# A four-layer trunk on one Trainium2 core: the RWKV chains of four tiles become two chains of two tiles in step

## The chip, the cores and the metric

The kernel runs on one core of a Trainium2 chip. Its engines are TensorE (PE, matmuls, with its weight loads as a row of their own, PEld), VectorE (DVE), ScalarE (ACT), GpSimd (POOL) and SyncE (SP), whose queue issues the DMAs. The metric is the device time of one execution, in microseconds. The time before is the median of three runs, and beside it stands one execution taken with the hardware profiler, from which all rows come.

## What is computed

Two layers of a decoder trunk on 256 positions of width 2048, each followed by a SwiGLU FFN, all between RMS norms, in float32. The second layer is an RWKV-7 time mix with 32 heads of 64. Its heart is a recurrence over the positions (cut from the reference):

```python
def step(state, inp):
    r_t, d_t, k_t, v_t, kk_t, a_t = inp
    sk = jnp.einsum("bhvk,bhk->bhv", state, kk_t)
    state = (state * d_t[:, :, None, :]
             - sk[..., None] * (kk_t * a_t)[:, :, None, :]
             + v_t[..., None] * k_t[:, :, None, :])
    return state, jnp.einsum("bhvk,bhk->bhv", state, r_t)
...
y = ((y - mu) * lax.rsqrt(var + RWKV_LN_EPS)).reshape(b, s, d)
y = y * ln_w + ln_b
bonus = jnp.sum(r_h * k_h * r_k, axis=-1, keepdims=True) * v_h
return ((y + bonus.reshape(b, s, d)) * gate) @ w_o
```

## The kernel before

The recurrence is computed in chunks of 64 positions (four of them), for a tile of 128 channels (two heads) at a time: 16 tiles, eight pairs q of two tiles, four groups g of two pairs. All this is one stage of the kernel, some 490 us long, in which several kinds of work are woven together:

- `rec_pre(q)` projects receptance and key of a pair (lines 1294 to 1299): 2 x 16 blocks of 6 matmuls into a `pw` bank each, evacuated by ScalarE into `r_t` (L1296, two buffers) and `k_t` (L1298, one buffer). The weights come as `raw` by DMA (L371, three buffers) and are split into `whi` (ScalarE, L273) and `wlo` (VectorE, L274).
- `rec_load(q)` loads four prepared tensors of the pair, `rec_head(q)` makes from them and `r_t`, `k_t`, for each tile, `KR`, `BK`, `AB`, `KG`, `BT` and `V` (L1349 to L1397). `KR`, `AB`, `KG`, `V` and `BT` have five buffers (`NH = 5`), `BK` has one. Its matmuls go to the three banks of tag `ph`.
- `rec_solve(g)` is the chain of a group of four tiles. It inverts triangular matrices by doubling: for each of four levels two steps, each with 64 matmuls of 32 x 32 (`mul`, L1413; the profile has two records of each), evacuated by VectorE (`W`, L1427), or by ScalarE and VectorE (`Tm`, `Rc`, L1431 and L1432). Two joins follow (L1439, L1450), and then the four chunks in turn: `X` (L1466, L1469, evacuated by ScalarE at L1471), `E` (L1476, L1477), and the state `S` (L1488, L1490, L1492 or L1494). At the end come the outputs of the two pairs, one after the other (L1509 to L1535): matmuls, a norm over each head, the bonus and the gate (L1531). The chain's matmuls go to the three banks of tag `pc`; its tiles `R`, `Rc`, `Tm`, `W`, `X` and `S` have one buffer each.
- `rec_gate(q)` loads the pair's gate into `gt` (one buffer, L1544).
- `wo_part(i)` adds part of the output projection (first of tiles 0 to 7, then of 8 to 11), with two `pw` banks at a time (L317, L322, L323). The last part follows after the stage.

PSUM has eight banks: two of `pw`, three of `ph`, three of `pc`. The tasks get due times: pair q's projections from q - 1.6 to q - 0.55, its head from q - 0.5 to q + 0.45, group g's chain from 2g + 1.5 for `LS` = 1.5, its gates `LS` - 0.5 behind; `weave` runs them step by step in the order of these times. From the order in which they are written and a model of the engines, the library then sets the order on every engine, which is fixed when the kernel is built. In it an instruction that is written earlier goes first among those that are ready.

Of the kernel before, what the change touches and what calls it, by code (L numbers as in the profile page):

```python
# [11 lines left out]
F32 = mybir.dt.float32  # L12
# [91 lines left out]
def tile_trunk(ctx: ExitStack, tc: tile.TileContext, A, out, dbg=None):  # L104
# [1156 lines left out]
    rebank(2, {"ph": 3, "pc": 3})  # L1261
    rcx, rcp = phase("rec")
    RB = {"r_t": 2, "KR": NH, "AB": NH, "KG": NH, "V": NH, "BT": NH, "bon": 3, "pd": 2}
# [137 lines left out]
    def rec_solve(g):  # L1401
# [3 lines left out]
        U4 = range(4)  # L1405
        UC = [(u, ch) for u in U4 for ch in range(4)]

        def mul(L, X):

            v_ = c32(pbank("pc"))  # L1410
            for u, ch in UC:
                for b, s_ in enumerate(QS):
                    mm(v_[s_, 4 * u + ch, :], lhsT=L(b, u, ch), rhs=X[s_, 4 * u + ch, :], start=True, stop=True)  # L1413
            return v_


        Rw = Sr([P, 16, 64], "R")
        for u in U4:
            tt(Rw[:, 4 * u : 4 * u + 4, :], AB[u][:, :, 0:64], bcn("rm1t", 4), ALU.mult)
        R = Sr([P, 16, 32], "Rc")  # L1420
        tt(R, Rw[:, :, 0:32], Rw[:, :, 32:64], ALU.add)
        Tm = Sr([P, 16, 32], "Tm")
        nc.vector.transpose(flat(Tm), flat(R))
        for lv in (2, 4, 8, 16):
            W = Sr([P, 16, 32], "W")
            p_ = mul(lambda b, u, ch: AB[u][QS[b], ch, 32 * (b % 2) : 32 * (b % 2) + 32], Tm)
            tt(W, p_, bcn(f"rl{lv}", 16), ALU.mult)  # L1427
            yield 1
            p_ = mul(lambda b, u, ch: R[QS[b], 4 * u + ch, :], W)
            Tm, R = Sr([P, 16, 32], "Tm"), Sr([P, 16, 32], "Rc")  # L1430
            act(flat(Tm), flat(p_), AF.Copy)  # L1431
            nc.vector.transpose(flat(R), flat(p_))  # L1432
            yield 1

        Rc, R = R, Sr([P, 16, 64], "R")
        p_ = c32(pbank("pc"))
        for u, ch in UC:
            for b in (0, 2):
                mm(p_[QS[b + 1], 4 * u + ch, :], lhsT=AB[u][QS[b], ch, 32:64], rhs=Tm[QS[b], 4 * u + ch, :],  # L1439
                   start=True, stop=True)  # L1440
        W = Sr([P, 16, 32], "W")
        act(W[QS[1]], p_[QS[1]], AF.Copy)
        nc.vector.tensor_copy(W[QS[3]], p_[QS[3]])
        tt(R.rearrange("p c (b n) -> p c b n", b=2), Rc.unsqueeze(2).to_broadcast([P, 16, 2, 32]),
           C("bd32").rearrange("p (b n) -> p b n", b=2).unsqueeze(1).to_broadcast([P, 16, 2, 32]), ALU.mult)
        yield 1
        p_ = c32(pbank("pc"))
        for u, ch in UC:
            for b in (0, 2):
                mm(p_[QS[b], 4 * u + ch, :], lhsT=W[QS[b + 1], 4 * u + ch, :], rhs=Rc[QS[b + 1], 4 * u + ch, :],  # L1450
                   start=True, stop=True)
        act(R[QS[0], :, 32:64], p_[QS[0]], AF.Copy)
        nc.vector.tensor_copy(R[QS[2], :, 32:64], p_[QS[2]])
        yield 1

        Ss = Sr([P, 3, 4, 64], "S")
        E2 = [Sr([P, 2, 4, 64], t) for t in ("Tm", "Rc")]

        def E(ch):
            return E2[ch // 2][:, ch % 2]  # L1460

        for ch in range(4):
            px = c64(pbank("pc")[:, :T])
            for u in U4:
                for s_ in HS:
                    mm(px[s_, u, :], lhsT=KG[u][s_, ch, 0:64], rhs=V[u][s_, ch, :], start=True, stop=ch == 0)  # L1466
                if ch:
                    for s_ in HS:
                        mm(px[s_, u, :], lhsT=KR[u][s_, ch, 0:64], rhs=Ss[s_, ch - 1, u, :], start=False, stop=True)  # L1469
            X = Sr([P, 4, 64], "X")  # L1470
            act(X, px, AF.Copy)  # L1471
            yield 1
            pe = c64(pbank("pc")[:, :T])
            for u in U4:
                for s_ in HS:
                    mm(pe[s_, u, :], lhsT=R[s_, 4 * u + ch, :], rhs=X[s_, u, :], start=True, stop=True)  # L1476
            nc.vector.tensor_copy(E(ch), pe)  # L1477
            if ch in (1, 2):
                dec = Sr([P, 4, 64], "X")
                for u in range(2):  # L1480
                    tt(dec[:, 2 * u : 2 * u + 2, :], Ss[:, ch - 1, 2 * u : 2 * u + 2, :],
                       pds[u][:, :, ch].unsqueeze(2).to_broadcast([P, 2, 64]), ALU.mult)
            yield 1
            if ch < 3:
                pS = c64(pbank("pc")[:, :T])
                for u in U4:
                    for s_ in HS:
                        mm(pS[s_, u, :], lhsT=BT[u][s_, ch, 1, :], rhs=V[u][s_, ch, :], start=True, stop=False)  # L1488
                    for s_ in HS:
                        mm(pS[s_, u, :], lhsT=BT[u][s_, ch, 0, :], rhs=E(ch)[s_, u, :], start=False, stop=True)  # L1490
                if ch:
                    tt(Ss[:, ch], dec, pS, ALU.add)  # L1492
                else:
                    nc.vector.tensor_copy(Ss[:, 0], pS)  # L1494
                yield 1
        for v in range(2):
            pr2 = 2 * g + v
            py = pbank("pc")
            y4 = py.rearrange("p (u c n) -> p u c n", u=2, n=64)
            for w_ in range(2):  # L1500
                u = 2 * v + w_
                for i in range(3):
                    for ch in range(4):
                        if i == 1 and ch == 0:
                            continue
                        for s_ in HS:
                            lhs, rhs = ((V[u][s_, ch, :], KG), (Ss[s_, max(ch - 1, 0), u, :], KR),
                                        (E(ch)[s_, u, :], AB))[i]
# [8 lines left out]
            r0, sq = flat(Sr([P, 2, T], "W")), Sr([P, 2, 2 * T], "R")[:, 0, :]  # L1517
            act(r0, pv, AF.Abs_reciprocal_sqrt, bias=epst[:, 2:3], scale=1.0 / 64)
            act(sq, r0, AF.Square)
            yield 1  # L1520
            stt(sq, pv, 64 * 64e-5, sq, ALU.add, ALU.mult)
            act(sq, sq, AF.Copy, scale=-0.5 / 64, bias=1.5)
            tt(r0, py, r0, ALU.mult)
            tt(r0, r0, sq, ALU.mult)
            for j in range(2):
                c = 2 * pr2 + j
# [64 lines left out]
    for g in range(4):  # L1591
        t = 2 * g + 1.5
        tasks.append((t, t + LS, 28, rec_solve(g)))
# [51 lines left out]
```

## Time and profile before

| | |
|---|---|
| time, median of three runs | 2665.96 us (2663.95 to 2678.07) |
| profiled execution | 2662.39 us, of which the span from first to last instruction 2660.6 us |
| mean granted TensorE clock | 0.978 of 2.4 GHz |
| PE busy | 2569.1 us (97% of the span) |
| PEld, DVE, ACT busy | 2225.8, 1540.4, 1315.0 us |
| the stage of the change | about 1397 to 1891 us after the span's start |

Busy time of PE counts a matmul until its modelled end. Idle time of an engine is put down to what released the instruction that follows it: another engine's line, a DMA, or "issue", where the profile shows no releaser.

### The profile page before, as it was taken

What the parts mean: (1) busy time and instruction counts of PE and PEld (TensorE: products, weight loads), DVE (VectorE), ACT (ScalarE), POOL (GpSimd) and SP (SyncE); (2) the same over time, 40 slices, a digit from 0 to 9 for tenths busy, and PEclk for the clock granted to TensorE, in tenths of its full rate; (3) what the DMA queues carried; (4) which work ended last, traced back from release to release, by engine and by line L of the source; (5) the groups of instructions that cost most, each with busy time, mean ns of one, the idle gap of its engine ahead of it and who ended that gap; (6) DMA issues with size and microseconds to landing.
All of it is one profiled execution on the core that took longest, in us unless ns stands there. A gap on an engine that the chain in (4) does not pass through costs nothing.

```text
span 2660.6 us, 50321 instructions
## 1 busy us (share of the span) xinstructions
PE 2569.1 (97%) x21102; PEld 2225.8 (84%) x21102; DVE 1540.4 (58%) x2183; ACT 1315.0 (49%) x1953; POOL 33.3 (1%) x99
## 2 busy tenths in 40 slices
PE   8999999999999999998999998889899999999998
PEld 8999988788888888887999897777688888888886
DVE  7866666655444554458776574664655444555455
ACT  6665545544444434445577473553554444443443
POOL 1000000000000000000000000000000000000000
PEclk9999999999999999998999998899899999999999
DMA  7544546666566656655587442533366666666665
GB/s 208 148 121 129 175 144 198 179 185 194 183 192 187 193 187 190 190 186 176 177 278 219 130 133 67 171 99 126 112 185 190 190 192 193 187 193 194 190 184 164
DMA packets 275331, 461.49 MB, mean 173 GB/s; under 512 B 23752, under 2 KB 89216, under 8 KB 274336
## 3 DMA queue, kind: packets, MB, share of 16 engines
q1 hardware_dynamic: 274720, 458.12, 56.6%
q8 instruction: 165, 2.70, 0.4%
q14 instruction: 62, 0.51, 0.1%
q0 software_dynamic: 384, 0.16, 0.0%
HBM read 441.93 MB, written 16.29 MB: 172 GB/s over the span
## 4 chain that ended last, share of the span: by engine, by line
PE 92%; DVE 3%; ACT 2%; DMA 2%; issue 1%; SPq 0%; DVEq 0%; ACTq 0%
PE pw L317 27%; PE pw L322 20%; PE pw L323 20%; PE pw L320 7%; PE pw L319 7%; PE pc L1413 2%; PE ph L1364 1%; PE pc L1509 1%; DVE wlo L274 1%; DMA raw<-in_rwkv_w_o_dram 1%; PE pc L1476 1%; ACT whi L273 1%; PE pw L1176 1%; PE pc L1490 0%; PE pc L1469 0%
## 5 line engine op out<-in xcount | busy, mean ns | idle before, releaser
L274 DVE TENSOR_TENSOR wlo<-raw,whi 128x1024 fp32r<-128x1024 f32 (+1 forms) x814 | 975.9, 1201 | 881.1 <-ACT whi L273 877.4
L273 ACT ACTIVATE whi<-raw 128x1024 fp32r<-128x1024 f32 (+1 forms) x814 | 844.4, 1040 | 971.3 <-PE pw L323 795.9
L322 PE MATMUL pw<-wlo,xs_hi 128*128 128x512 f32 x1664 | 651.9, 392 | 0.0
L323 PE MATMUL pw<-whi,xs_lo 128*128 128x512 f32 x1664 | 648.8, 391 | 0.0
L317 PE MATMUL pw<-whi,xs_hi 128*128 128x512 f32 x1664 | 599.6, 393 | 0.7 <-ACT fw L465 0.7
L322 PEld LDWEIGHTS pw<-wlo,xs_hi 128*128 128x128 f32 x1664 | 313.6, 188 | 65.0 <-issue 0.7
L317 PEld LDWEIGHTS pw<-whi,xs_hi 128*128 128x128 f32 x1664 | 313.1, 188 | 65.5 <-issue 1.0
L323 PEld LDWEIGHTS pw<-whi,xs_lo 128*128 128x128 f32 x1664 | 313.2, 188 | 65.3 <-issue 0.7
L317 PE MATMUL pw<-xs_hi,whi 128*128 128x256 f32 x1168 | 334.1, 288 | 4.2 <-ACT xs_hi L1148 3.6
L319 PE MATMUL pw<-xs_lo,whi 128*128 128x256 f32 x1168 | 332.5, 286 | 0.0
L320 PE MATMUL pw<-xs_hi,wlo 128*128 128x256 f32 x1168 | 329.7, 287 | 0.3 <-DVE wlo L274 0.3
L323 PE MATMUL pw<-whi,hidl 128*128 128x512 f32 x704 | 276.7, 393 | 0.0
L322 PE MATMUL pw<-wlo,hidh 128*128 128x512 f32 x704 | 275.9, 392 | 0.0
L317 PE MATMUL pw<-whi,hidh 128*128 128x512 f32 x704 | 250.2, 393 | 0.0
L317 PEld LDWEIGHTS pw<-xs_hi,whi 128*128 128x128 f32 x1168 | 224.1, 192 | 6.0 <-ACT xs_hi L1148 3.9
L319 PEld LDWEIGHTS pw<-xs_lo,whi 128*128 128x128 f32 x1168 | 224.0, 192 | 0.9 <-DVE xs_lo L1138 0.3
L320 PEld LDWEIGHTS pw<-xs_hi,wlo 128*128 128x128 f32 x1168 | 221.9, 192 | 1.2 <-DVE wlo L274 0.5
L323 PEld LDWEIGHTS pw<-whi,hidl 128*128 128x128 f32 x704 | 132.3, 188 | 30.0
L317 PEld LDWEIGHTS pw<-whi,hidh 128*128 128x128 f32 x704 | 132.3, 188 | 29.3
L322 PEld LDWEIGHTS pw<-wlo,hidh 128*128 128x128 f32 x704 | 132.3, 188 | 29.0
L320 PE MATMUL pw<-xr_hi,wlo 128*128 128x256 f32 x288 | 82.1, 285 | 2.4 <-DVE wlo L274 2.3
L317 PE MATMUL pw<-xr_hi,whi 128*128 128x256 f32 x288 | 82.1, 285 | 2.0 <-ACT whi L273 2.0
(582 smaller groups left out, 2502.0 us busy)
## 6 DMA issues: line engine op xcount, KB each, us to landing
raw<-in_ffn_w_gate_dram SPq DMA_DIRECT2D x176, 512.0 KB, 3.8
raw<-in_ffn_w_up_dram SPq DMA_DIRECT2D x176, 512.0 KB, 3.7
raw<-in_ffn_w_down_dram SPq DMA_DIRECT2D x176, 512.0 KB, 3.7
raw<-in_hyb_w_in_dram SPq DMA_DIRECT2D x80, 512.0 KB, 3.7
raw<-in_hyb_w_out_dram SPq DMA_DIRECT2D x32, 512.0 KB, 3.9
raw<-in_rwkv_w_v_dram SPq DMA_DIRECT2D x32, 512.0 KB, 4.4
raw<-in_rwkv_w_r_dram SPq DMA_DIRECT2D x32, 512.0 KB, 4.5
raw<-in_rwkv_w_k_dram SPq DMA_DIRECT2D x32, 512.0 KB, 4.2
```

Source lines behind the costliest of these rows:

```text
L273: behind(act(hi, src, AF.Copy), after[0])
L274: behind(tt(lo, src, hi.bitcast(F32), ALU.subtract), after[1])
L317: mm(dst, lhsT=lh, rhs=rh, start=start, stop=False, skip_group_check=True)
L319: mm(dst, lhsT=lh, rhs=rl, start=False, stop=False, skip_group_check=True)
L320: mm(dst, lhsT=ll, rhs=rh, start=False, stop=stop, skip_group_check=True)
L322: mm(dst, lhsT=lh, rhs=rl, start=False, stop=False, skip_group_check=True)
L323: mm(dst, lhsT=ll, rhs=rh, start=False, stop=stop, skip_group_check=True)
L1176: mm(ps[:96, 0, :], lhsT=wt[:, (c + j) % 8, :], rhs=xm[:, j, :], start=c + j == 0, stop=c + j == ND - 1)
L1364: mm(g[:, ch * P : (ch + 1) * P], lhsT=bdk[:, ch, i, :], rhs=KR[:, ch, :], start=True, stop=True)
L1413: mm(v_[s_, 4 * u + ch, :], lhsT=L(b, u, ch), rhs=X[s_, 4 * u + ch, :], start=True, stop=True)
L1476: mm(pe[s_, u, :], lhsT=R[s_, 4 * u + ch, :], rhs=X[s_, u, :], start=True, stop=True)
L1509: mm(y4[s_, w_, ch, :], lhsT=lhs, rhs=rhs[u][s_, ch, 64:128], start=i + ch == 0, stop=i == 2, skip_group_check=True)
```

## The change

Each group's chain becomes two chains, of two tiles each, which are written step by step in turn. Each has its own tiles (`R0`, `R1` and so on, half as wide) and its own two PSUM banks (`pc0`, `pc1`); `ph` has two banks left. All matmuls stay; each evacuation is half as wide, and there are twice as many. The outputs of both pairs are written in turn as well, each by single tiles of 256 columns: squares and head sums in `W`, `Tm` and `Rc`, then the norm, the bonus and, for both tiles together, the gate. The key gets a second buffer. The gate loads use the one buffer of `BK` in place of `gt`. A chain's slot `LS` is 1.3 in place of 1.5, and its instructions count as if they were written 100 places earlier.

```diff
-    rebank(2, {"ph": 3, "pc": 3})
+    rebank(2, {"ph": 2, "pc0": 2, "pc1": 2})
-    RB = {"r_t": 2, "KR": NH, "AB": NH, "KG": NH, "V": NH, "BT": NH, "bon": 3, "pd": 2}
+    RB = {"k_t": 2, "r_t": 2, "KR": NH, "AB": NH, "KG": NH, "V": NH, "BT": NH, "bon": 3, "pd": 2}
...
+        R, Ss, E = [None, None], [None, None], [None, None]
+        def chain(v):
+            UC = [(u, ch) for u in range(2) for ch in range(4)]
+            ab, kr, kg, bt, vv = (x[2 * v : 2 * v + 2] for x in (AB, KR, KG, BT, V))
+            pc = f"pc{v}"
+            def Sv(shape, tag, dt=F32):
+                return Sr(shape, tag + str(v), dt)
...
-            W = Sr([P, 16, 32], "W")
-            p_ = mul(lambda b, u, ch: AB[u][QS[b], ch, 32 * (b % 2) : 32 * (b % 2) + 32], Tm)
-            tt(W, p_, bcn(f"rl{lv}", 16), ALU.mult)
+                W = Sv([P, 8, 32], "W")
+                p_ = mul(lambda b, u, ch: ab[u][QS[b], ch, 32 * (b % 2) : 32 * (b % 2) + 32], Tm)
+                tt(W, p_, bcn(f"rl{lv}", 8), ALU.mult)
...
-            X = Sr([P, 4, 64], "X")
-            act(X, px, AF.Copy)
+                X = Sv([P, 2, 64], "X")
+                act(X, px, AF.Copy)
...
-            sq = Sr([P, 2, T], "W")
-            act(flat(sq), py, AF.Square)
-            pv = pbank("pc")
-            hl = Sr([P, 2, 2 * T], "R", F32R)
-            headsum(pv, flat(sq), hl[:, 0, :], hl[:, 1, :])
...
+            pv = pbank(pc)
             for j in range(2):
+                sl = slice(j * T, (j + 1) * T)
+                sq = Sv([P, T], "W")
+                act(sq, py[:, sl], AF.Square)
+                headsum(pv[:, sl], sq, Sv([P, T], "Tm", F32R), Sv([P, T], "Rc", F32R))
+            yield 1
+            for j in range(2):
+                sl = slice(j * T, (j + 1) * T)
                 c = 2 * pr2 + j
+                r0, sq = Sv([P, T], "W"), Sv([P, T], "Tm")
+                act(r0, pv[:, sl], AF.Abs_reciprocal_sqrt, bias=epst[:, 2:3], scale=1.0 / 64)
+                act(sq, r0, AF.Square)
+                stt(sq, pv[:, sl], 64 * 64e-5, sq, ALU.add, ALU.mult)
+                act(sq, sq, AF.Copy, scale=-0.5 / 64, bias=1.5)
+                tt(r0, py[:, sl], r0, ALU.mult)
+                tt(r0, r0, sq, ALU.mult)
+                act(r0, r0, AF.Identity, scale=pcol(3, 32 + c), bias=pcol(3, 48 + c))
+                tt(bon[:, sl], r0, bon[:, sl], ALU.add)
             tt(bon, bon, flat(gate[pr2]), ALU.mult)
...
+        for f in (chain, output):
+            for _ in zip(f(0), f(1)):
+                yield 1
...
-        gate[pr2] = Sr([P, 2, T], "gt")
+        gate[pr2] = Sr([P, 2, T], "BK")
...
-    LS = 1.5
+    LS = 1.3
...
-        tasks.append((t, t + LS, 28, rec_solve(g)))
+        tasks.append((t, t + LS, 28, rec_solve(g), 100))
```

## Rows read from the trace of the kernel before

**Rows 1.** Stretch, length, busy us of PE, PEld, DVE, ACT, POOL; clock; DMA share, GB/s.

```profile
1472.10:1579.70 107.60, 101.45 (x2221) 95.14 (x2220) 69.94 (x110) 62.06 (x111) 4.78 (x12) 1.00 0.41 126
1579.70:1689.70 110.00, 99.15 (x2153) 92.67 (x2151) 64.50 (x103) 57.14 (x106) 4.05 (x12) 0.91 0.38 117
1689.70:1795.40 105.70, 89.16 (x1931) 76.20 (x1930) 58.72 (x93) 51.56 (x97) 4.12 (x12) 0.87 0.36 114
1795.40:1884.20 88.80, 75.81 (x1761) 62.82 (x1761) 39.79 (x53) 28.41 (x39) 0.00 (x0) 0.87 0.31 99
...
1612.60:1644.80 32.20, 22.64 (x593) 20.14 (x593) 9.35 (x19) 3.79 (x8) 0.31 (x2) 0.68 0.09 27
```

**Rows 2.** Chain of waits in order of time (start, us): first output matmuls of each chain.

```profile
1534.78 1.87 PE pc L1509 x64
...
1642.98 1.87 PE pc L1509 x64
...
1748.87 1.87 PE pc L1509 x64
...
1869.46 3.46 PE pc L1509 x88
```

**Rows 3.** PE's timeline (start, us, what): projections around the first chain's end.

```profile
1520.85 0.28 PE L319 MATMUL pw<-xr_lo,whi 128*128 128x256 f32 x1
1520.97 0.28 PE L320 MATMUL pw<-xr_hi,wlo 128*128 128x256 f32 x1
...
1540.53 0.39 PE L317 MATMUL pw<-xs_hi,whi 128*128 128x256 f32 x1
```

**Rows 4.** Timeline of VectorE and ScalarE at the first chain's output matmuls.

```profile
1535.64 0.43 DVE L1349 TENSOR_TENSOR KR<-r_t,Pt 128x256 f32<-128x256 f32 x1 [0.39 <-PE pc L1509]
...
1536.10 0.60 ACT L1296 ACTIVATE r_t<-pw 128x512 f32<-128x512 f32 x1 [2.06 <-DVE KR L1349]
1536.59 0.59 ACT L1298 ACTIVATE k_t<-pw 128x512 f32<-128x512 f32 x1
```

**Rows 5.** Timelines of PE and ScalarE in the third chain: output projection and last key.

```profile
1709.60 0.40 PE L323 MATMUL pw<-whi,xs_lo 128*128 128x512 f32 x1
...
1750.53 0.60 ACT L1298 ACTIVATE k_t<-pw 128x512 f32<-128x512 f32 x1 [2.39 <-DVE KR L1350]
...
1754.62 0.50 PE L317 MATMUL pw<-whi,xs_hi 128*128 128x512 f32 x1
```

**Rows 6.** ScalarE's timeline, two chunks; PE's waits of L1476 (us, times, longest).

```profile
1529.33 0.38 ACT L1471 ACTIVATE X<-pc 128x256 f32<-128x256 f32 x1 [3.94 <-PE pc L1469]
1533.66 0.38 ACT L1471 ACTIVATE X<-pc 128x256 f32<-128x256 f32 x1 [3.94 <-PE pc L1469]
...
PE pc L1476 <- ACT X L1471: 6.9, 13, 0.5
```

**Rows 7.** PE's timeline in level steps of chains 1 and 2; PE's waits of L1413.

```profile
1618.03 1.17 PE L1439 MATMUL pc<-Tm,AB 32*32 32x32 f32 x36 [0.77 <-ACT Tm L1431]
...
1710.41 0.44 PE L1413 MATMUL pc<-Tm,AB 32*32 32x32 f32 x28 [0.41 <-ACT Tm L1431]
...
1715.10 1.59 PE L1413 MATMUL pc<-W,Rc 32*32 32x32 f32 x100 [1.47 <-issue]
...
1724.65 0.57 PE L1439 MATMUL pc<-Tm,AB 32*32 32x32 f32 x13 [0.74 <-ACT Tm L1431]
...
PE pc L1413 <- issue: 11.2, 15, 2.3
```

**Rows 8.** VectorE's timeline after the first chain; landing of the gate loads (line 1544).

```profile
1549.92 0.42 DVE L1352 TENSOR_TENSOR BK<-r,pis 128x256 f32<-128x256 f32 x1
...
1577.56 0.68 DVE L1531 TENSOR_TENSOR bon<-bon,gt 128x512 f32<-128x512 f32 x1
...
DMA to landing us min/median/max: 2.7/4.0/8.8
```

**Rows 9.** VectorE's timeline: the first pair's split in the last chain.

```profile
1883.49 0.69 DVE L274 TENSOR_TENSOR xs_lo<-bon,xs_hi 128x512 fp32r<-128x512 f32 x1
```

More of the change, by code (lines that the diff above doesn't have):

```diff
@@ L1404, in rec_solve @@
         pds, bons = zip(*(heads.pop(("pair", 2 * g + u)) for u in range(2)))
[L1405 to L1410, printed above, removed]
-            for u, ch in UC:
[L1412 to L1424, printed above, removed]
-            W = Sr([P, 16, 32], "W")
-            p_ = mul(lambda b, u, ch: AB[u][QS[b], ch, 32 * (b % 2) : 32 * (b % 2) + 32], Tm)
-            tt(W, p_, bcn(f"rl{lv}", 16), ALU.mult)
-            yield 1
[L1429 to L1432, printed above, removed]
-            yield 1
@@ L1435, in rec_solve @@
[L1435 to L1467, printed above, removed]
-                    for s_ in HS:
-                        mm(px[s_, u, :], lhsT=KR[u][s_, ch, 0:64], rhs=Ss[s_, ch - 1, u, :], start=False, stop=True)
-            X = Sr([P, 4, 64], "X")
-            act(X, px, AF.Copy)
[L1472 to L1479, printed above, removed]
-                for u in range(2):
[L1481 to L1486, printed above, removed]
-                    for s_ in HS:
[L1488 to L1494, printed above, removed]
-                yield 1
@@ L1497, in rec_solve, with output, Sv @@
+        def output(v):
             pr2 = 2 * g + v
-            py = pbank("pc")
+            pc = f"pc{v}"
+            def Sv(shape, tag, dt=F32):
+                return Sr(shape, tag + str(v), dt)
+            py = pbank(pc)
             y4 = py.rearrange("p (u c n) -> p u c n", u=2, n=64)
@@ L1506, in rec_solve @@
                         for s_ in HS:
-                            lhs, rhs = ((V[u][s_, ch, :], KG), (Ss[s_, max(ch - 1, 0), u, :], KR),
-                                        (E(ch)[s_, u, :], AB))[i]
+                            lhs, rhs = ((V[u][s_, ch, :], KG), (Ss[v][s_, max(ch - 1, 0), w_, :], KR),
+                                        (E[v](ch)[s_, w_, :], AB))[i]
                             mm(y4[s_, w_, ch, :], lhsT=lhs, rhs=rhs[u][s_, ch, 64:128], start=i + ch == 0, stop=i == 2,
@@ L1538, in rec_solve @@
             yield 1
+        for f in (chain, output):
+            for _ in zip(f(0), f(1)):
+                yield 1
     box, heads, gate, done = {}, {}, {}, set()
     def rec_gate(pr2):
-        gate[pr2] = Sr([P, 2, T], "gt")
+        gate[pr2] = Sr([P, 2, T], "BK")
         nc.sync.dma_start(gate[pr2], gts[:, 2 * pr2 : 2 * pr2 + 2, :])
```

78 lines of the change are left out of this document (66 added, 12 removed).

## The prediction, made before the changed kernel had run

> **What bounds the kernel now.** I read busy time and clock by stretch first, from one chain's first matmul to the next one's (the last stretch ends where the output projection resumes) [rows 1]. TensorE (PE) is busy for 365.6 of these 412.1 us. So the part can shorten only by time in which PE stands still and time in which it runs at its lower level. Stretch length less PE's busy time gives 6.2, 10.9, 16.5 and 13.0 us of idle, 46.5 us in all. Granted clocks of 1.00, 0.91, 0.87 and 0.87 mean that 0, 20, 27 and 23 us passed at 1.2 instead of 2.4 GHz, 70 us in all. The low time lies where PE had been idling: of the 32.2 us from 1612.6 on PE was busy for 22.6, a share of 0.70, at a clock of 0.68. At that share the low level costs 70 x 0.70 / 2 = 25 us. So the ceiling of any gain is 46.5 + 25 = 71 us.
>
> Why does PE stand still? The chain of waits in order of time dates the first output matmuls (L1509) of each chain [rows 2]. With the starts [rows 1], the chains run for 62.7, 63.3, 59.2 and 74.1 us, and 44.9, 46.7 and 46.5 us pass from there to the next chain's start, in which PE is full of projections and heads. While a chain runs, projections fill its waits until they run out. The first chain shows why they do: the last projection matmul starts at 1521.0, the next at 1540.5 [rows 3]. Only when the first output matmuls have released a KR buffer does the waiting head write its second KR (L1349, its end releases r_t), and r_t and k_t are evacuated right behind it [rows 4]. Five KR buffers hold one group of four tiles and one more, so head 2g+2 stops after its first tile until the output of g begins. It keeps its r_t and the only k_t; the next key projection cannot leave its bank, and the one after cannot begin. In the third chain that is the last key: its bank is kept until k_t's evacuation at 1750.5, and the output projection, which wants both `pw` banks, stops at 1710.0 and resumes at 1754.6 [rows 5]. Without fill PE follows the chain: from X to X 4.33 us [rows 6].
>
> **The change part by part.**
>
> *Second k_t buffer.* Key 2g+3 is evacuated at once, so one more key projection (16 blocks x 6 matmuls = 96, at 0.12 us from start to start [rows 3], 11.5 us) can run in the naked parts of chains 0 and 1. In chain 2 the last key leaves its bank 40 us or more earlier, and the output projection goes on there. No work is removed; idle time is filled, at most 6.2, 10.9 and 16.5 us of it. Late next: r_t has two buffers, so the receptance projection behind that key still stops.
>
> *Two chains of two tiles.* The matmuls stay the same in number and size; every evacuation is halved and doubled. While one chain is evacuated, the other has PE. A chain has three parts:
> (a) Eight level steps of 128 matmul records and as many weight loads. With fill they take 4.79 us each (from 1579.7 to the join at 1618.0, by eight); naked 3.56 us (1710.41 to 1724.65, by four), with up to 1.47 us of "issue" in a step, in which PE waits for nothing that the profile shows [rows 7]. Halved evacuations do nothing for that, so 3.56 is the lower and 4.79 the upper bound; I take the middle, 4.2, hence 33.6 us.
> (b) The two joins (L1439, L1450): from the join to the outputs 1618.0 to 1643.0 and 1724.7 to 1748.9 [rows 2, 7], less four chunks of 4.33, leaves 7 us; I take 5, with one evacuation hidden in each.
> (c) Four chunks, now 4.33 us each when naked. Three handoffs are in one; that of X takes 6.9 / 13 = 0.53 us [rows 6], so PE's own work is 2.75 us or a little more. Two chains in step lie between; I take 3.5, hence 14 us.
> Sum 52.6 us. Against now that is 10.1, 10.7, 6.6 and 21.5 us less. The first is capped by the idle of its stretch, 6.2, because PE is otherwise full there; I take 6. In the last chain output projections are laid between the steps now; with most of them spent in chain 2, I expect it to run like the others. Sum: 6 + 10.7 + 6.6 + 21.5 = 44.8 us.
>
> *Doubled evacuations.* On ScalarE 512 columns take 0.59 us [rows 4] and 256 take 0.38 [rows 6]: a doubled one costs 0.17 us more; on VectorE 0.68 and 0.42 [rows 8], 0.16 us more. With about 20 and 31 per chain: 3.4 and 5 us. ScalarE is idle for 45.5 us of the first stretch and VectorE for 37.7 [rows 1], beside a busy PE, so I take nothing. Without that cover: 4 x 5 = 20 us.
>
> *Outputs by single tiles, both pairs in step.* In the last chain, now: from 1869.5 to the end of the first pair's split at 1884.2, 14.7 us [rows 2, 9]. The new first pair runs two single tiles in a row through one W buffer, and shares its engines with the other pair. PE resumes on the first pair: +1 us, between -3 and +6.
>
> *Gate in the BK buffer.* BK has one buffer, which now passes from the waiting head's second tile to gate 2g, to gate 2g+1, and then to head 2g+3: that head waits for both outputs. Now it writes BK at 1549.9, while the second output is multiplied by its gate only at 1577.6, 43 us after the outputs began [rows 2, 8]. New: release after KR, BK, bdk and BC, some 5 us; a gate load of 4.0 us (2.7 to 8.8) [rows 8]; a product; a second load; a product: 15 us at best, about as long as the head waits today (1534.8 to 1549.9). I take no change. The other bound is that 43 us: 28 us later per stretch. On SP's queue the weight loads behind a waiting gate load wait with it; three raw buffers cover 3 x 24 matmuls x 0.12 us = 8.6 us.
>
> *The rest.* `ph` with two banks instead of three: hidden by projections; without them one evacuation of 0.68 us [rows 8] for each of four products of a head, 22 us for eight heads. The lead of 100 places and the shorter slot put a chain's evacuations ahead of weight splits on ScalarE and VectorE, which work in order: where a chain step is late, splits wait behind it, and so does PE's fill. Bounds by one evacuation: 0 to 0.7 us a step; taken as 0, since 4.2 us includes the fill. The renamed buffers cost nothing.
>
> Total 44.8 - 1 = 43.8 us. The profiled execution took 2662.4 us (span 2660.6): 2662.4 - 43.8 = 2618.6, rounded to 2619. The shown median, 2666.0, lies 3.6 us above it; that is left in the range.
>
> **A rule against one of these rows.** PE's matmuls of L1413 lost 11.2 us to "issue" in 15 places of this part, 0.75 us each [rows 7], and among the matmuls of the chains these waits sit where small instructions come densest. The Trainium skill, "Runtime: NRT & Kernel Launch", section on instruction fetch mechanics, holds that instruction fetch is hidden, since dispatch is slower than the refill; by it a level step would have no such floor, and the sum would be that of rival 2.
>
> **The rivals.**
> 1 (slower). The BK ring decides. If the second gate product stays 43 us after the outputs begin, head 2g+3 starts 28 us later in three stretches, 84 us; the deeper store of keys covers 11.5 us in each of the first two. That leaves 61: 2662.4 - 43.8 + 61 = 2680. The ring eats the whole gain from about 15 us per stretch, that is, when the product comes later than 30 us. For: one buffer, and two loads in series behind outputs that took that long. Against: today's outputs share single W and R buffers and come behind the heads; the new ones lead by 100 places.
> 2 (much faster). Nothing binds but PE. Level steps lose their issue time (3.56 - 0.75 = 2.8 us; 8 x 1.4 = 11 us less per chain), and the sum goes to the ceiling: 2662.4 - 71 = 2591. Against: the rows of "issue".
> 3 (smaller). Level steps stay at 4.79 us, and the last chain keeps its 74 us because fill is laid into it as before. What is left is half of the idle of chains 0 to 2, 17 us: 2645.
> 4 (no difference). The order written out puts one chain behind the other: each half step still waits for its evacuation, now twice. The 17 us of fill are spent on 20 us of doubled evacuations: 2665.
>
> **How the numbers follow.** Forecast 2619 (2600 to 2637): 58%. Rival 2: 11%. Rival 3: 14%. Rival 4: 8%. Rival 1: 9%. The range leaves out rival 1, rival 4 and the tail beyond rival 2: 2590 to 2656. A measurement of this kernel can tell about 0.5% (13 us) from no change. Faster: the forecast, rival 2 and most of rival 3, 0.81. Same: the rest of rival 3 and rival 4, 0.10. Slower: rival 1, 0.09.
>
> **What would show it.** Right: projections between the chunks of chains 0 and 1, output projections between those of chain 2; X to X below 4 us; stretches with a clock near 1.00; chains near 53 us. The BK ring shows in the distance from a chain's first output matmuls to the next chain's start (46 us now). Wrong: that distance above 60 us, more issue time in the L1413 steps, or a last chain above 70 us.

## The result, and the profile after

The changed kernel takes 2691.99 us (median of six runs, 2686.10 to 2696.04) beside 2666.55 us for the kernel before on the same chip: a ratio of 1.0089 with a 95% interval of 1.0067 to 1.0110. It is slower by some 25 us where 44 us less was forecast, and it lies outside the range. The profiled execution took 2693.55 us (span 2691.7), 31 us more than that of before.

Busy time and clock by stretch, as in [rows 1]: stretch, length, busy us of PE, PEld, DVE, ACT, POOL, clock, DMA share, GB/s. The first row starts at the same 1472.1, although the first chain's first matmul now comes at 1459.4. The stretch that took 412.1 us before, to where the output projection resumes, now ends at 1914.6.

```profile
1472.10:1587.20 115.10, 112.39 (x2125) 102.41 (x2123) 60.78 (x113) 53.21 (x104) 3.18 (x8) 0.94 0.33 101
1587.20:1696.00 108.80, 105.16 (x2163) 95.98 (x2163) 66.42 (x129) 59.47 (x123) 5.86 (x12) 0.95 0.38 116
1696.00:1820.00 124.00, 115.70 (x2047) 95.48 (x2048) 75.92 (x141) 70.72 (x142) 5.86 (x12) 0.94 0.44 142
1820.00:1914.60 94.60, 81.65 (x1777) 67.29 (x1778) 47.15 (x95) 34.38 (x74) 2.58 (x4) 0.79 0.22 66
...
1475.00:1485.00 10.00, 10.00 (x202) 7.68 (x191) 4.28 (x9) 3.62 (x9) 0.00 (x0) 0.68 0.20 61
```

PE stands still for 27.6 us of these 442.5, against 46.5 us of 412.1 before. So the idle time did shrink; but PE is busy for 414.9 us in place of 365.6. Only a little of that is more work: this window holds 8103 matmul records in place of 8062, and 54 more 128x256 projection matmuls among them are 6.5 us at 0.12 us each. The last row shows where to look: ten microseconds without a gap, at a clock of 0.68. The groups of PE by line, for the same stretch, name the work that grew (busy us, mean ns of one), first of the changed kernel, then of the kernel before:

```profile
L1421 PE MATMUL pc<-Tm,AB 32*32 32x32 f32 x1984 | 39.6, 206 | 3.7 <-DVE Tm L1431 2.4 <-issue 0.8 <-ACT Tm L1439 0.4
L1421 PE MATMUL pc<-W,Rc 32*32 32x32 f32 x2048 | 34.0, 200 | 3.8 <-issue 2.9 <-DVE W L1435 0.9
...
L1394 PE MATMUL ph<-cst,v_t 64*64 64x64 f32 x224 | 23.0, 242 | 0.0
```

```profile
L1413 PE MATMUL pc<-Tm,AB 32*32 32x32 f32 x2048 | 23.0, 196 | 4.8 <-issue 3.7 <-ACT Tm L1431 1.2
L1413 PE MATMUL pc<-W,Rc 32*32 32x32 f32 x2048 | 24.5, 200 | 10.0 <-issue 7.5 <-DVE W L1427 2.2
...
L1394 PE MATMUL ph<-cst,v_t 64*64 64x64 f32 x192 | 6.9, 221 | 0.0
```

The two groups of level steps (L1413, now L1421) were busy for 23.0 and 24.5 us and are now for 39.6 and 34.0; the v_t product (L1394) was for 6.9 us and is now for 23.0. A matmul by itself is at most a tenth longer (206, 200 and 242 ns in the mean, against 196, 200 and 221). PE's timeline (start, us, line, out<-in, tile size) shows that the two now take turns.

```profile
1474.82 0.48 PE L1421 MATMUL pc<-W,Rc 32*32 32x32 f32 x33
1475.23 0.33 PE L1394 MATMUL ph<-cst,v_t 64*64 64x64 f32 x2
1475.48 0.24 PE L1421 MATMUL pc<-W,Rc 32*32 32x32 f32 x2
1475.66 0.32 PE L1394 MATMUL ph<-cst,v_t 64*64 64x64 f32 x2
```

One turn of two and two records takes 0.43 us (1475.23 to 1475.66). In [rows 7] a run of 28 such 32x32 records takes 0.44 us.

The chunks of the first chain are another matter. X of the one half comes at 1529.70 and 1539.59, X of the other at 1534.07 and 1543.93 (ScalarE's timeline), 9.9 us from X to X of a half where 4.33 were measured before [rows 6] and 3.5 forecast. But the 4.33 us stood without other work between them, and here PE is full, as its row for this time shows: busy for 14.23 of 14.23 us at the full clock, with some 70 projection matmuls among the records. This is the fill between the chunks that was forecast for this chain; the 9.9 us are no loss by themselves.

```profile
1529.70 0.28 ACT L1476 ACTIVATE X<-pc 128x128 f32<-128x128 f32 x1 [2.89 <-PE pc L1471]
1534.07 0.27 ACT L1476 ACTIVATE X<-pc 128x128 f32<-128x128 f32 x1
1539.59 0.28 ACT L1476 ACTIVATE X<-pc 128x128 f32<-128x128 f32 x1 [2.03 <-PE pc L1474]
1543.93 0.28 ACT L1476 ACTIVATE X<-pc 128x128 f32<-128x128 f32 x1 [2.51 <-PE pc L1474]
...
1529.70:1543.93 14.23, 14.23 (x207) 12.94 (x207) 6.47 (x13) 6.35 (x13) 0.00 (x0) 1.00 0.34 106
```

**Where the time stands, by kernel.** I split the stretch from 1380.0 us to the first matmul of the next stage (tile `pA`) into five parts, from PE's records in order of start. Idle is every gap over 150 ns in which neither a matmul nor a weight load runs ("issue" is the part with no releaser). Low clock is half of what remains of the time at the 1.2 GHz level. A change of size is a record whose tile size (32x32, 64x64 or 128 rows) differs from the one before; its price is the time from start to start, put to the full clock, less what the record takes in a run of its own size (9 ns, 30 ns, or the median of its form). The rest is the matmuls' own time. All in us, each from the one profiled execution, so some us of a row are chance (the one of e_lead20k lies 9 us under its median).

| kernel | stretch | idle | of it issue | low clock | changes of size | the rest |
|---|---|---|---|---|---|---|
| before | 534.1 | 55.9 | 12.8 | 31.4 | 13.0 (128) | 433.7 |
| changed | 565.0 | 37.4 | 5.4 | 38.1 | 47.6 (431) | 441.9 |
| changed, no lead (e_lead0) | 539.4 | 60.0 | 19.8 | 21.9 | 20.4 (210) | 437.0 |
| changed, lead 20000 (e_lead20k) | 513.4 | 23.1 | 4.0 | 14.3 | 37.2 (342) | 438.8 |
| two chains without lead, ring and second key (e_a0_gt_k1) | 549.3 | 67.7 | 40.2 | 30.1 | 18.5 (182) | 432.9 |
| before, gate in BK (e_gate) | 553.5 | 67.6 | 16.7 | 38.6 | 12.0 (117) | 435.4 |

The stretch explains the whole difference: 30.9 us against 31 between the two executions. Idle gave 18.5 us back; changes of size took 34.6, the low clock 6.7 and the rest 8.2. In every row a change costs 0.10 to 0.11 us. Of the 8.2 us of the rest, about 1 is 9 projection matmuls that the kernel before had done ahead of 1380.0; what the others are stays open.

### The profile page after: what moved, and what is told of

It reads as the page before. It is cut to its first block, busy times and chain, and to the rows that moved or that the text cites. A ratio compares the mean times of both kernels' runs of the same rounds, so it can differ in the third digit from the quotient of the medians.

```text
span 2691.7 us, 50625 instructions
## 1 busy us (share of the span) xinstructions
PE 2618.4 (97%) x21118; PEld 2256.7 (84%) x21118; DVE 1554.8 (58%) x2303; ACT 1328.4 (49%) x2033; POOL 37.5 (1%) x99
## 4 chain that ended last, share of the span: by engine, by line
PE 92%; DVE 2%; ACT 2%; DMA 2%; issue 1%; SPq 0%; DVEq 0%; ACTq 0%
PE pw L317 27%; PE pw L323 20%; PE pw L322 20%; PE pw L320 7%; PE pw L319 7%; PE pc L1421 2%; PE ph L1364 1%; DVE wlo L274 1%; PE ph L1394 1%; PE pc L1518 1%; ACT whi L273 1%; PE pw L1176 1%; PE pc L1471 0%; DMA yg<-ygs 0%; PE pc L1481 0%
## 5 line engine op out<-in xcount | busy, mean ns | idle before, releaser
L273 ACT ACTIVATE whi<-raw 128x1024 fp32r<-128x1024 f32 (+1 forms) x814 | 844.4, 1040 | 964.8 <-PE pw L323 780.0
```

Of the source, the lines that this page charges most:

```text
L273: behind(act(hi, src, AF.Copy), after[0])
```

## The experiments

Three theories were put against each other. S: changes of tile size on PE, multiplied by the two half chains and by the lead of 100 places, are what the time went into. R: the gate in the BK buffer holds the heads (rival 1 of the prediction); below this wait is called the ring. L: the lead itself harms, by putting the chains ahead of other work. Times are given as ratios to the kernel before on the same chip, with the 95% interval; 0.001 is 2.7 us.

| run | ratio | interval |
|---|---|---|
| changed kernel | 1.0089 | 1.0067 to 1.0110 |
| e_lead0 | 1.0013 | 1.0002 to 1.0024 |
| e_lead20k | 0.9954 | 0.9936 to 0.9973 |
| e_before_lead | 1.0041 | 1.0025 to 1.0057 |
| e_before_lead20k | 0.9990 | 0.9975 to 1.0005 |
| e_gate | 1.0060 | 1.0044 to 1.0077 |
| e_key2 | 1.0067 | 1.0052 to 1.0082 |
| e_a0_gt_k1 | 1.0047 | 1.0032 to 1.0063 |
| e_a_gt_k1 | 1.0110 | 1.0095 to 1.0126 |
| e_gateR | 1.0105 | 1.0090 to 1.0120 |
| e_lead0_ls15 | 1.0069 | 1.0053 to 1.0086 |
| e_lead0_k1 | 1.0005 | 0.9993 to 1.0017 |
| e_full_gt_k1 | 0.9974 | 0.9965 to 0.9983 |
| e_full_k1 | 0.9949 | 0.9936 to 0.9962 |
| e_full_gateR | 0.9952 | 0.9939 to 0.9965 |

### The price of a change of size

`e_sizes` is the kernel before with blocks of small matmuls behind its end:

```diff
+    for f, nf, g, ng, times in (
...
+        (size32, 64, size64, 32, 1), (size32, 16, size64, 8, 4), (size32, 4, size64, 2, 16), (size32, 1, size64, 1, 64),
...
+        block(f, nf, g, ng, times)
```

> The kernel before with 14 blocks of small matmuls behind its end, in a chain of one block after the other, to price a change of tile size by itself: 64 matmuls of 32x32 and 32 of 64x64, first all of the one and then all of the other (1 change), then in turns of 16 and 8, of 4 and 2, of 1 and 1; the same for 32x32 with 128x128 and 64x64 with 128x128; and as a control turns of one size between two PSUM banks. Theory S: a block without alternation takes about 128 x 12.5 ns + 64 x 37 ns = 4 us; each change adds 0.1 to 0.25 us, so 31 changes add 3 to 8 us and turns of 1 and 1 over 20 us; the control costs no more than a block of one size. Rival W (what cost time in the changed kernel were waits on evacuations or the change of bank, not the size): alternation adds under 0.03 us a change, or the control costs as much as the alternation.

The turns of 4 and 2 matmuls (8 and 4 records) on PE's timeline, then the turns of 1 and 1:

```profile
2675.96 0.26 PE L1629 MATMUL pc<-mby,mba 32*32 32x32 f32 x8
2676.15 0.33 PE L1632 MATMUL ph<-mby,mba 64*64 64x64 f32 x4
2676.42 0.26 PE L1629 MATMUL pc<-mby,mba 32*32 32x32 f32 x8
...
2689.99 0.31 PE L1629 MATMUL pc<-mby,mba 32*32 32x32 f32 x2
2690.23 0.47 PE L1632 MATMUL ph<-mby,mba 64*64 64x64 f32 x2
2690.63 0.31 PE L1629 MATMUL pc<-mby,mba 32*32 32x32 f32 x2
```

And busy time and clock of three stretches: the turns of 4 and 2 matmuls in two parts, and the turns of 1 and 1.

```profile
2675.96:2679.20 3.24, 3.24 (x93) 2.48 (x92) 0.69 (x1) 0.42 (x1) 0.00 (x0) 1.00 0.02 5
2679.80:2684.60 4.80, 4.80 (x94) 3.53 (x92) 0.00 (x0) 0.00 (x0) 0.00 (x0) 0.50 0.02 3
2685.51:2726.00 40.49, 40.49 (x254) 29.03 (x254) 0.50 (x1) 0.42 (x1) 0.00 (x0) 0.50 0.00 1
```

A turn of 12 records takes 0.46 us (2675.96 to 2676.42) at the full clock. By the 9 and 30 ns at which records of one size follow each other (128 of 32x32 from 2663.69 to 2664.91; 512 of 64x64 in 15.4 us in `e_dense`) it would take 0.19. So a change between these two sizes costs 0.13 us, with no wait and no evacuation in it. To and from 128x256 matmuls it costs more:

```profile
2750.39 0.26 PE L1629 MATMUL pc<-mby,mba 32*32 32x32 f32 x8
...
2750.90 0.26 PE L1629 MATMUL pc<-mby,mba 32*32 32x32 f32 x8
...
2766.20 0.33 PE L1632 MATMUL pc<-mby,mba 64*64 64x64 f32 x4
...
2766.78 0.33 PE L1632 MATMUL pc<-mby,mba 64*64 64x64 f32 x4
```

A turn of 8 records of 32x32 and one of 128x256 takes 0.51 us, a turn of 4 of 64x64 and one of 128x256 takes 0.58; with 0.12 us for a 128x256 matmul their own time is 0.19 and 0.24, so a change costs 0.16 and 0.17 us. At the low level a turn of 1 and 1 takes 0.64 us (2689.99 to 2690.63) for four records. And the clock falls under such turns although PE, by the modelled ends of its matmuls, is busy the whole time: 3.24 of 3.24 us at 1.00, then 4.80 of 4.80 and 40.49 of 40.49 at 0.50. Theory S holds in the price, and the turns also bring the low level that I had tied to idle time alone. The control, turns between two banks in one size, shows no such step: 215 records of 32x32, in turns of one to eight between the banks, take 3.0 us at the low level, 14 ns each.

The Trainium skill, "TensorEngine Tiling (Array Packing)", section "Key Properties", has the rule that I should have set against this change: "Changing tiling mode (not just tile) drains the TensorE". It gives no price; the rows put it at 0.13 to 0.17 us in these blocks, and at 0.10 to 0.11 in the table above.

### The lead

```diff
-        tasks.append((t, t + LS, 28, rec_solve(g), 100))
+        tasks.append((t, t + LS, 28, rec_solve(g)))            # e_lead0
+        tasks.append((t, t + LS, 28, rec_solve(g), 20000))     # e_lead20k
```

`e_before_lead` and `e_before_lead20k` add a lead of 100 and of 20000 places to the kernel before.

> The changed kernel without the lead of 100 places for the chains, nothing else undone: two chains, second key buffer, gate in the BK buffer, single-tile outputs and two ph banks stay. Theory S (tile size): TensorE loses time wherever the next matmul in its order has another tile size (32x32 in the level steps, 64x64 in the chunks, 128x128 in projections and heads). From the two traces: in the RWKV part 123 changes of size before, 392 after, at some 0.2 us from start to start, against 12 to 40 ns between records of one size; the lead lets the chains' matmuls alternate with v_t, heads and projections in ones and twos. As written out, this kernel's order has 207 changes and the changed kernel's 428: 221 fewer, 0.15 to 0.2 us each, 33 to 44 us less than the changed kernel, 2648 to 2659 us. Rival B (gates in the BK ring): the chains' outputs come later without the lead, the second gate product with them, 2690 to 2720. Rival C (halved and doubled evacuations, more and smaller instructions): these are all still there, 2687 to 2697, as the changed kernel.

> The kernel before with the lead of 100 places for its one chain, nothing else. The order written out has 130 changes of tile size, the kernel before 123. Theory S: within 0.3% of before, 2660 to 2672 us, since what costs is the alternation and not the lead. Rival L (the lead itself: chain evacuations stand ahead of weight splits on ScalarE and VectorE and hold up the fill, up to 0.7 us in each of some 28 steps of four chains): up to 78 us slower; 2680 or more.

> The changed kernel with a lead of 20000 places in place of 100: a chain's block is taken whole as soon as its operand is there, instead of in turns with heads and projections whose places overlap with it. Written order: 340 changes of tile size (428 with 100, 207 without a lead). The blocks of small matmuls run by themselves price a change at 0.11 us (to or from 32x32 and 64x64) to 0.19 us (from 128x128), and alternation pulled the clock down. Theory S (changes of size are what the lead costs): 88 fewer, 9 to 15 us less, and some of the low clock back: 2670 to 2684 us. Rival L (standing ahead of the others is what costs): a larger lead costs as much or more, 2690 or more.

> The kernel before with a lead of 20000 places for its one chain, nothing else. Two chains with that lead took 2650 us. Theory T (it is the two chains that keep TensorE supplied, the lead only keeps their blocks whole): one chain with the lead stays a chain in which TensorE waits between steps, 2665 to 2685 us, as with the lead of 100 (2677). Rival L2 (a whole lead is enough by itself): 2640 to 2655.

Without the lead the changed kernel takes 2669.07 us, 23 us less (20 by the ratios), where 33 to 44 less was expected: the sign, and half to two thirds of the size. By the table 27 us of changes and 16 us of low clock go away, but 23 us of idle come back; I read that as chains that no longer find their way between the projections. The lead of 100 costs 18 us without the ring and the second key too (`e_a_gt_k1` against `e_a0_gt_k1`, below) and 11 us in the one-chain kernel, where it adds hardly a change (135 for 128). Its 2677.21 us lie between the ranges of S and L. Counted as in the table, its stretch is 15.4 us longer than before, of which 7.7 are idle (3.8 of them issue) and 3.8 low clock. So something of theory L is left; why the idle time grows is open.

The lead of 20000 is the surprise: 2650.38 us, 42 us less than with 100 (36 by the ratios), faster than both kernels. Not the standing ahead costs, but standing ahead by a little. A step of the two half chains writes 64 matmuls and their evacuations; moved up by 100 places its numbers fall among those of heads written shortly before, and the two are then taken in turns. That explanation is read from the written order, not measured. The rows show that with 20000 a half chain's block is whole, 64 records between projections, one step 3.72 us after the other, and without a wait:

```profile
1554.48 0.28 PE L320 MATMUL pw<-xr_hi,wlo 128*128 128x256 f32 x1
1554.69 0.75 PE L1421 MATMUL pc<-Tm,AB 32*32 32x32 f32 x64
1555.37 0.38 PE L317 MATMUL pw<-xr_hi,whi 128*128 128x256 f32 x1
...
1558.41 0.75 PE L1421 MATMUL pc<-W,Rc 32*32 32x32 f32 x64
...
1570.10 0.69 PE L1447 MATMUL pc<-Tm,AB 32*32 32x32 f32 x32
...
1604.21 0.66 PE L1447 MATMUL pc<-Tm,AB 32*32 32x32 f32 x30
```

The last two rows are the joins (L1447) of the two halves of this group. They show that the halves do not run in step: the level steps of the one end at 1570.1, those of the other start at 1574.6 and end at 1604.2, beside the first half's chunks, and the outputs begin at 1616.0 and 1646.5. In all four groups of this kernel the joins of the halves start 26 to 45 us apart: two halves in step are not how it gains.

Of the 51.6 us between the two stretches in the table, changes of size are 10.4; 23.8 are the clock and 14.3 idle. So S as I put it, a sum of changes, expected 2670 to 2684 and was too small by 20 us; the accounting shows the parts, no run separates them. One chain with the same lead is the kernel before again (0.9990): the lead is not enough by itself, the two chains earn the 13 us.

### The gate in BK, and the second key

```diff
-        gate[pr2] = Sr([P, 2, T], "gt")
+        gate[pr2] = Sr([P, 2, T], "BK")      # e_gate; e_key2 adds "k_t": 2
```

> The kernel before with the gate loaded into the one BK buffer and nothing else (one k_t, one chain, no lead). In the run of the second key together with the gate in BK, the first BK after a chain's first output matmuls came 34 us behind them (before: 3 us), the last head's KR 49 us behind (before: 30), and the time was 18 us over before. Theory R (the ring: head 2g+3 waits for both gate products): this alone is enough, 2676 to 2695 us, and the first BK after the outputs is again over 25 us behind them. Rival K (the second k_t does the harm: keys evacuated early take ScalarE or the order from something else): the gate alone changes nothing, 2660 to 2672.

> The kernel before with a second k_t buffer and the gate loaded into the BK buffer, nothing else: one chain of four tiles, no lead. 122 changes of tile size as written out, 123 before. Theory S: no slower than before; the fill of idle stretches gives 0 to 17 us: 2649 to 2668 us. Rival B (the second gate product holds BK and with it the next pair's head, 28 us in each of three stretches): slower, 2690 or more, since outputs are as late as before.

In the one-chain kernel theory R is right: the gate in BK alone costs 16 us. A head writes BK in two parts, L1351 and L1352. VectorE's timeline of `e_gate`, whose first output matmuls are at 1538.8:

```profile
1556.27 0.69 DVE L1531 TENSOR_TENSOR bon<-bon,BK 128x512 f32<-128x512 f32 x1
1570.15 0.68 DVE L1531 TENSOR_TENSOR bon<-bon,BK 128x512 f32<-128x512 f32 x1
1570.87 0.43 DVE L1351 TENSOR_TENSOR BK<-kh,ip 128x256 f32<-128x256 f32 x1
1571.21 0.42 DVE L1352 TENSOR_TENSOR BK<-r,pis 128x256 f32<-128x256 f32 x1
```

Both parts of the next head's BK follow the second product at once, 32 us after the outputs began. Before, the first part came at 1537.94, 3 us after the outputs, and the second at 1549.92 [rows 8], 15 us after them, and the second product came later. The second key buffer adds nothing to it (1.0067 beside 1.0060); the 2683.44 us of `e_key2` lie between its two ranges.

In the changed kernel the ring is as plain: the second product at 1593.81, the next BK right behind it, 39 us after the outputs began at 1555.9.

```profile
1586.72 0.69 DVE L1542 TENSOR_TENSOR bon<-bon,BK 128x512 f32<-128x512 f32 x1
1593.81 0.69 DVE L1542 TENSOR_TENSOR bon<-bon,BK 128x512 f32<-128x512 f32 x1
1594.54 0.42 DVE L1351 TENSOR_TENSOR BK<-kh,ip 128x256 f32<-128x256 f32 x1
```

But there it costs nothing, as these five show. `e_a0_gt_k1` and `e_a_gt_k1` give the gate its own buffer again (and k_t one), without the lead and with the lead of 100; `e_gateR` loads it into the R buffer of its own chain, without the lead; `e_lead0_k1` and `e_lead0_ls15` are `e_lead0` with one k_t and with the slot of 1.5.

```diff
-        gate[pr2] = Sr([P, 2, T], "BK")
+        gate[pr2] = Sr([P, 2, T], "gt")      # e_a0_gt_k1, e_a_gt_k1
+            gate[pr2] = Sv([P, 2, T], "R")   # e_gateR, at the head of output()
```

> The changed kernel with the gate in a buffer of its own again (so k_t has one, for lack of room) and without the lead: two chains, split outputs and two ph banks alone. Theory R: the ring costs some 18 us in the changed kernel too, so this is that much under the changed kernel without its lead (2669): 2645 to 2658, faster than before. Rival: the ring is hidden in the two-chain kernel, whose first chain needs the first pair of heads only; then 2665 to 2675.

> The changed kernel with the gate in a buffer of its own (and one k_t), its lead of 100 kept: 468 changes of tile size in the written order, 428 in the changed kernel, 179 without the lead. If ring and lead add up: the changed kernel (2692) less the ring's 18 us, 2668 to 2680, and 20 to 30 us above the same kernel without the lead. If the alternation matters only because late heads are squeezed beside the chains (the ring as its cause): 2645 to 2660, near the kernel without the lead.

> The changed kernel without the lead and with the gate loaded into the R buffer of its own chain, which is free once that chain's last E matmul is done and is wanted next by the next group's chain: two chains, two k_t, no ring with the heads; 169 changes of tile size in the written order. Theory R plus S: what is left is the gain that was forecast, less what some 45 changes more than before cost (at 0.11 to 0.3 us each, as the blocks of small matmuls show, 5 to 13 us): 2635 to 2652 us. If the gain of two chains was never there: 2660 or more.

> The changed kernel without the lead and with one k_t; the gate stays in the BK buffer. With ring and two k_t it took 2669 us, with neither 2679. If the second key buffer is what makes the difference: 2675 to 2685. If it is the gate in BK, which holds the second pair's head back until projections have been laid beside the first chain: 2664 to 2672.

> The changed kernel without the lead and with the slot of 1.5 of before in place of 1.3, so that a chain's steps are spread over more of the fill in the written order. 214 changes of size (207 with 1.3). If the shorter slot costs (chains run out of fill, and the level steps stand bare with their issue time): 2652 to 2664 us. If it does not matter: 2665 to 2673, as with 1.3.

Three of the five came out beside every value expected of them (`e_a0_gt_k1`, `e_a_gt_k1`, `e_lead0_ls15`); `e_gateR` fell where the gain of two chains was never there (2660 or more), and `e_lead0_k1`, at 2663.88 us, on the edge of its second range. Taking the ring away made the kernel without a lead slower by 10 us (2679.18; 15 us beside `e_lead0_k1`, which has one key buffer too) and 26 us (2695.13), and with the lead of 100 it changed nothing that the intervals can tell (1.0110 beside 1.0089). The table says where: `e_a0_gt_k1` has 40.2 us of issue. Its waits of PE, and PE's timeline in the third chain:

```profile
PE pc L1421 <- issue: 37.9, 20, 5.1
...
1718.64 1.88 PE L1421 MATMUL pc<-Tm,AB 32*32 32x32 f32 x124 [5.11 <-issue]
...
1722.11 1.87 PE L1421 MATMUL pc<-W,Rc 32*32 32x32 f32 x124 [1.54 <-issue]
...
1725.59 1.87 PE L1421 MATMUL pc<-Tm,AB 32*32 32x32 f32 x124 [1.55 <-issue]
```

The level steps of both halves stand bare, one behind the other, 3.47 us each, and 1.5 us of that is issue. The heads come earlier without the ring (the second part of the first BK after the first chain at 1560.7, in `e_lead0` at 1578.9), the projections are then spent before the chain, and the chain has nothing between its steps. (That the projections go first is my reading of the traces; no run moves them alone.) The shorter slot, which I had bounded as a loss, gains: 1.5 in place of 1.3 costs 11 us without the lead (2679.83 us; 15 by the ratios).

### What a bare level step waits for

`e_dense` has four long blocks behind the end of the kernel before:

```diff
+        (size32, 512, size32, 512, 1), (size64, 256, size64, 256, 1), (size128, 64, size128, 64, 1),
+        (size32, 32, size128, 16, 16),
```

> The kernel before with four long blocks behind its end, to price TensorE's supply of instructions: 1024 matmuls of 32x32 (2048 records and as many weight loads), 512 of 64x64, 128 of 128x256, and 16 turns of 32 matmuls of 32x32 and 16 of 128x256. Theory F (bare level steps are bound by the supply of instructions: 128 records in 3.5 us, 27 ns each, with issue time between short runs of 8 to 13 ns): the first block takes 50 to 60 us, the 64x64 block 28 to 40 us, and in the mixed block the supply is hidden (16 x 2.8 = 45 us). Rival (the issue time in the level steps comes from semaphores of the evacuations): the first block runs at 8 to 13 ns a record throughout, 17 to 27 us.

PE's timeline in the first block, and the DMA queues for 2669 to 2709 us (packets, MB, share of 16 engines):

```profile
2665.46 1.27 PE L1629 MATMUL pc<-mby,mba 32*32 32x32 f32 x128 [2.75 <-issue]
2669.21 1.92 PE L1629 MATMUL pc<-mby,mba 32*32 32x32 f32 x128 [2.47 <-issue]
2672.95 1.93 PE L1629 MATMUL pc<-mby,mba 32*32 32x32 f32 x128 [1.82 <-issue]
2676.43 1.93 PE L1629 MATMUL pc<-mby,mba 32*32 32x32 f32 x128 [1.54 <-issue]
...
q8 instruction: 11, 0.18, 1.7%
```

No evacuation, no other engine: 128 matmul records and their 128 weight loads, then a wait, every 3.47 to 3.75 us, and one instruction packet of 16 KB (0.18 MB / 11) in each 3.6 us. The first row is still at the full clock: its records take 1.27 us in place of 1.93, the wait before it is 2.75 us in place of 1.5 to 1.8, and the next run starts 3.75 us later all the same. The whole block takes 56.3 us, within the 50 to 60 expected. Theory F holds: a bare level step is bound at some 3.5 us for 256 instructions, at the pace of the instruction packets. In the last block, 64 records between 16 of 128x256, the turns of 2.78 us show no such wait (41.1 of 41.1 us busy at clock 1.00), as expected; projections laid between hide it. So the rule that I set against [rows 7] (the Trainium skill, "Runtime: NRT & Kernel Launch", section "Instruction fetch mechanics", by which the fetch is hidden) holds between projections and fails for runs of 32x32 matmuls.

### With the blocks kept whole

Lead 20000 with the three other forms of gate and key: `e_full_gt_k1` (gate in its own buffer, one k_t), `e_full_k1` (gate in BK, one k_t), `e_full_gateR` (gate in R, two k_t).

> Two chains with the lead of 20000, the gate in a buffer of its own and one k_t: neither ring nor second key. With both: 2650. Without a lead the kernel without ring and second key was 10 us slower than with both, with the lead of 100 6 us slower. If ring and key are indifferent or help here too: 2650 to 2662. If the ring costs its 16 us of the one-chain kernel: 2630 to 2640.

> Two chains with the lead of 20000, the gate in the BK buffer, one k_t. Without a lead one k_t was 5 us faster than two. If the second key buffer brings nothing: 2640 to 2652; if it carries fill into the chains as forecast (6 to 17 us): 2656 to 2667.

> Two chains with the lead of 20000 and two k_t, the gate in its own chain's R buffer: no ring with the heads. Without a lead this was 26 us slower than with the ring, because the projections were spent before the chain and its level steps stood bare. With the whole lead the chains' blocks are laid between projections as soon as they can be, so if the ring itself costs, this is the fastest: 2630 to 2645. If the ring holds the heads back to the chains' good here too: 2655 to 2680.

They take 2658.29, 2651.05 and 2651.01 us (the last between its two ranges); with ring and two keys it was 2650.38. Neither the ring nor the second key makes a difference of its own once a chain's block is taken whole; only the kernel with neither lies some 7 us above the others. The fastest of all, 0.5% under the kernel before, is any of the other three.

## Why the prediction was wrong

*"The matmuls stay the same in number and size; every evacuation is halved and doubled."* This is the step that failed. But for the head sums of the outputs (32 matmuls of 256 columns in place of 16 of 512) number and size are the same; the order is not. Each half chain puts its own block between the projections, so changes of size rise from 128 to 210 without a lead and to 342 with whole blocks, and the lead of 100 takes the blocks in turns (431). By the table that is 34.6 us more, where the sum had nothing. Of the level steps (part a) I gave only a duration, 33.6 us for eight; a price per block between other work was missing. In chains 1 to 3 they now take 56, 79 and 68 us from the first matmul to the last, other work between them included.

*The ceiling of 71 us* assumed that the low clock lies where PE idles. It does before [rows 1]; it does not after, where 1475 to 1485 is full and stands at 0.68. Of the idle time, 18.5 us did go as forecast, and the low clock, which should have followed it down, rose by 6.7 (both by the table).

*The lead, "taken as 0", bounds 0 to 0.7 us a step.* It costs 18 to 23 us in the two-chain kernel, and not by holding up splits: `e_lead20k` stands further ahead and is 42 us faster.

*Two chains, 10 + 10.7 + 6.6 + 21.5 us less, capped to 44.8.* With neither lead nor ring nor second key, but with the split outputs, two `ph` banks and the slot of 1.3, they are 12 us slower than before (1.0047). Nor are the two in step, as part (c) had them: the joins of the halves start 11 us apart in the first chain (1512.4 and 1523.7). The lower bound of a level step, 3.56 us, was right to 0.1 us and was the trap: it is the price of a bare step, and a fill that has left a chain must be done elsewhere. Where fill stays between the steps, as with whole blocks, the mechanism shows: idle falls by 32.8 us and the low clock by 17.1, and changes and rest take 29.3 back; 20.7 us of the forecast 44 in that execution, 13 in the medians. The idle time can be won, but a third to a half of the forecast is left of it, and the lead as written hid it.

*Second key: 6 us or more.* Nothing, in any of three pairs (1.0067 and 1.0060; 1.0013 and 1.0005; 0.9954 and 0.9949), all three with the gate in BK; without that ring no pair differs in the key alone. That the receptance projection behind the key still stops, which I named as late next and did not price, would explain it; it was not tried.

*BK ring: 0, bound 28 us per stretch.* Right for the changed kernel's time, though not by the reason given: the ring closes 39 us after the outputs began, not 15. And [rows 8] were misread: the head did not wait for BK until 1549.9, since it had written the first part at 1537.94; the row is the second part. In the one-chain kernel it costs 16 us. So rival 1 named a real wait, which is not what made this kernel slow. Of the rivals none had the mechanism; rival 1, at 9%, had the sign.

*Outputs, +1 us, between -3 and +6.* From the first output matmuls of the last chain to the first projection matmul it is now 18.7 us, 4 more than before, within the bounds:

```profile
1895.94 0.57 PE L1518 MATMUL pc<-KG,V 64*64 64x64 f32 x14
...
1912.43 0.58 PE L1289 MATMUL pc<-Tm,bd64r 128*128 128x256 f32 x1 [4.80 <-ACT Tm L273]
...
1914.59 0.63 PE L317 MATMUL pw<-whi,xs_hi 128*128 128x512 f32 x1
```

The doubled evacuations were taken as 0: DVE and ACT are busy for 17 and 19 us more than in [rows 1], but of PE's 27.6 us of idle time only 6.5 end on evacuations of the chains; 12.4 end on the splits of the outputs (7.4 of them on `Tm`, L273). The two `ph` banks were not tried alone and stay open.

*The signs named.* The fill between the chunks came, and issue in the level steps fell from 11.2 to 3.8 us. From the first output matmuls to the next chain 31, 27 and 22 us pass instead of 45 to 47, so the sign of the ring did not show: work that stood between the chains has moved into them. One sign of being wrong did, the last chain: 75.9 us, above 70.

## What to carry to other kernels

Before splitting a chain of small matmuls, count on PE how often the tile size changes in the new order and give each change a measured price (0.10 to 0.17 us here); halving the blocks took the count from 128 to between 182 and 431. Of the leads tried here, 0, 100 and 20000 places, the one of 100, about one step's length, was the slowest in both kernels; in the kernel of two chains it made two kinds of work alternate. So try none, and one large enough that a block is taken whole. And a step's bare duration is no saving while the work that filled it must still be done: look at where the fill goes.

## What the runs showed of the hardware that was not expected

- A change between 32x32 and 64x64 matmuls cost 0.13 us at the full clock, one to or from 128x256 matmuls 0.16 to 0.17 us (`e_sizes`); turns of two records each ran at a clock of 0.50 for 40 us although PE was busy throughout by the profile.
- Runs of 32x32 matmuls are bound by the supply of instructions: 256 instructions every 3.47 to 3.75 us, with a wait of 1.5 to 1.8 us after each 128 matmul records at the low clock and of 2.5 to 2.8 us after 128 at the full one (`e_dense`). 512 matmuls of 64x64 did not show it so: 1024 records in 33.6 us, with one wait of 0.27 us; that is 256 instructions in 4.2 us, slower than the pace above.
